# Down-weight block sums in earlier places, and the last rows' roots on GpSimd, in a hybrid decoder block

## The chip, the cores and the metric

The kernel runs on one core of one Trainium2 chip. The metric is device time in microseconds (us). A core has engines with a queue each: TensorE (PE; its weight loads are PEld), VectorE (DVE), ScalarE (ACT), GpSimd (POOL) and SyncE (SP), which issues nearly all DMAs here. Each engine works its queue in order; engines wait for each other by semaphores, so an instruction that waits holds everything behind it on its own queue.

## The reference

A decoder block on 1024 tokens of width 1024, in float32: an S5 branch and a stick-breaking attention branch, merged, then a SwiGLU feed-forward layer, and a last norm. The change touches the end of the feed-forward layer and the last norm:

```python
def rmsnorm(x, g):
    xf = x.astype(jnp.float32)
    xf = xf * lax.rsqrt(jnp.mean(xf * xf, axis=-1, keepdims=True) + RMS_EPS)
    return (xf * g.astype(jnp.float32)).astype(x.dtype)

        ffn = (jax.nn.silu(h @ w_ffn_gate[l]) * (h @ w_ffn_up[l])) @ w_ffn_down[l]
        x = x + g2 * ffn
    return rmsnorm(x, norm_f_g)
```

The hidden width is 2816, so the down weights are 2816 x 1024. `g2` is a row of 1024 numbers that scales the columns of the down weights.

## The kernel before

**Products.** Every float32 product is made of three: an operand is cast to a shorter float on ACT (its high half, L473), and what is left is taken off on DVE (its low half, L474); high times high, high times low and low times high are summed in PSUM. `operand` does this "split" for a tile of 128x1024.

**Strassen.** The feed-forward products run as one level of Strassen: seven products of sums of half blocks in place of eight. The hidden columns are worked in eleven pairs of 256. Pairs 0 to 9 take the seven products; the eleventh is done plainly (`plain`), and its part of the down product comes last, row by row.

**Gate and up** (`gate_up`, once for each of ten pairs). After a pair's seven products (PE, L1279), ACT makes the silu (L1263), DVE the product with up (L1264), POOL five sums of half tiles (L1270), and SP stores seven left operands of the down product in `hD` (L1273). The tiles named f1 that hold them are used again by operands of the down product, once these stores have read them.

**Blocks of down weights.** The right operands of the down product come from the weights: for each pair, two tiles of 128x1024 are loaded (L1354; for the first four pairs L1194), scaled by `g2` on POOL (L1355, L1195), and combined into five sums of 128x512 on POOL (`down_sums`, L1326). Two scaled quarters are stored as they are (L1321) and the five sums in three stores (L1328). This is called a block here. Ten blocks, 0 to 9, are needed. Blocks 0 to 3 are made during gate and up, at every second pair; blocks 4, 5 and 6 beside products 3 to 5 of the first step of the down product; blocks 7, 8 and 9 beside products 3 to 5 of the second.

**The down product** (`down`). It has three steps, with four, three and three pairs each (`STEPS`); block q belongs to pair q, so the second step needs blocks 4 to 6 and the third blocks 7 to 9. In each step run the seven products (the first step in the order 2, 3, 1, 6, 7, 5, 4, the others in 2, 4, 5, 3, 1, 6, 7). A product has four row groups, each with 3 matmuls for every pair, summed in one PSUM bank (L1396): 48 matmuls in the first step, 36 in the others. For each pair of each product one operand is loaded from `hD` (L1375) into one of seven stage tiles (wb four times, ws twice, wgs), and split into one of eight pairs of tiles (named wh, wl, wgh, wxh, f). So there are 28, 21 and 21 operands. The results are copied (L1400) or added (L1402) to accumulators, and in the third step POOL combines these (`closing`, L1362).

**The last rows.** For eight rows of 128 tokens (4 to 7, then 0 to 3) PE adds the eleventh pair's part (L1433), DVE adds the accumulators (L1435), ACT sums squares (L1445; for the last row in halves, L1437), `rstd_s` makes the root with six ACT instructions on 128x1 (Ln, Exp, and one Newton step of four, L494 to L499), and DVE scales the row (L1418), which SP stores. The last row is scaled in halves, on ACT (L1412) and DVE (L1413); its first half is multiplied by the norm's weights on POOL beforehand (L1441), and its Ln takes a bias from the first half's sum, made by two small instructions (L1440).

**What sets the order.** A scheduler places the instructions on each queue when the program is built, from a model of their times. `after(a, b)` only tells it to place a behind b; at run time nothing waits for it. So the code's loops say when a block may be placed, and the scheduler where its parts stand on SP, POOL, DVE, ACT and PE.

## Time and profile before

| | |
|---|---|
| time, median of 3 runs | 1471.52 us (1470.78 to 1475.69) |
| the profiled execution: time, span of its instructions | 1475.07 us, 1473.3 us |
| busy in the span: PE, DVE, ACT, POOL | 1413.9, 1094.9, 632.8, 507.1 us |
| first matmul of the down product | 1243.71 us |
| first matmul of its second and third step | 1321.96 and 1379.08 us |
| first matmul of the last rows | 1440.74 us |
| blocks 4 to 9 on POOL, start to end | 1256.9 to 1273.9, 1278.0 to 1293.9, 1293.9 to 1311.8, 1311.8 to 1328.8, 1345.2 to 1361.1, 1361.1 to 1376.1 us |

A row of the order of time has the start, the length, the engine and the line, the operation, out<-in with the program's tile names, and in brackets the idle time of the engine before it, with who ended it. "SPq" is the issue of a DMA on SP's queue. A row of a window has its bounds and length, then the busy time and count of PE, PEld, DVE, ACT and POOL, the granted clock of TensorE, the share of the DMA engines and GB/s (with one engine alone where a row is shorter). A row of a group ends with the busy time, the mean length in ns, and the idle time before. A row of DMA issues ends with the size of one and the median time to landing. A matmul of 128x512 shows as 0.39 us, since matmuls overlap; they start some 0.227 us apart.

### The profile page before, as it was taken

How to read it: one execution, taken by the hardware profiler on the slowest of the kernel's cores; microseconds unless marked ns; L12 is line 12 of the kernel's file. 1: busy time of each engine (PE TensorE's matmuls, PEld its weight loads, DVE VectorE, ACT ScalarE, POOL GpSimd, SP SyncE). 2: the span in 40 equal slices, each digit the busy share in tenths (PEclk: the TensorE clock that was granted, in tenths of full speed). 3: DMA queues.
4: the chain of work that ended last, by engine and by line, in shares of the span. 5: the costliest groups of instructions: out<-in, count | busy, mean ns of one | idle time of the engine just before them, and what ended most of it. 6: DMA issues, size and time to landing. Idle time of an engine off the chain costs nothing.

```text
span 1473.3 us, 18281 instructions
## 1 busy us (share of the span) xinstructions
PE 1413.9 (96%) x6730; PEld 1118.4 (76%) x6730; DVE 1094.9 (74%) x1424; ACT 632.8 (43%) x847; POOL 507.1 (34%) x265
## 2 busy tenths in 40 slices
PE   5898999999899999999999999999999999999997
PEld 3678988788666666668888788888888888788785
DVE  5778996356788888887723678777766667999797
ACT  3321121641586858675418543233323234433335
POOL 1000000001210122102400015877667563895694
PEclk9999999999999999999999999999999999999998
DMA  9546664569311111116452223644444358999732
GB/s 339 140 104 157 161 178 120 173 199 335 109 36 51 36 51 57 50 50 218 141 198 88 85 86 108 208 147 167 137 133 146 124 197 315 328 340 330 277 102 115
DMA packets 193561, 233.39 MB, mean 158 GB/s; under 512 B 29500, under 2 KB 128896, under 8 KB 193472
## 3 DMA queue, kind: packets, MB, share of 16 engines
q1 hardware_dynamic: 184336, 224.70, 46.9%
q10 hardware_dynamic: 8912, 7.48, 1.9%
q8 instruction: 53, 0.87, 0.3%
q14 instruction: 36, 0.29, 0.1%
q0 software_dynamic: 224, 0.05, 0.0%
HBM read 162.85 MB, written 68.16 MB: 157 GB/s over the span
## 4 chain that ended last, share of the span: by engine, by line
PE 69%; DVE 13%; DMA 6%; ACT 5%; issue 3%; POOL 3%; SPq 1%; DVEq 0%; ACTq 0%; POOLq 0%
PE tq L1279 12%; PE mm L1279 6%; PE wo L1279 6%; PE mx L812 5%; PE ga L738 4%; PE mm L812 4%; PE mm L738 3%; PE acc L812 2%; PE mm L1117 2%; PE mm L646 2%; PE mx L738 2%; PE z L812 2%; PE wo L1117 2%; PE tq L1396 2%; PE tq L1228 2%
## 5 line engine op out<-in xcount | busy, mean ns | idle before, releaser
L471 POOL TENSOR_TENSOR ws<-wb 128x1024 f32<-128x1024 f32 x24 | 61.6, 2568 | 174.0 <-DVE wl L474 150.2
L455 POOL TENSOR_TENSOR wl<-ws,wh 128x1024 fp32r<-128x1024 f32 x12 | 31.3, 2610 | 166.7 <-ACT wh L452 166.2
L905 DVE TENSOR_TENSOR wa<-wa,acc 128x512 f32<-128x512 f32 (+1 forms) x80 | 47.0, 628 | 32.6 <-ACT row L903 30.1
L1270 POOL TENSOR_TENSOR f<-f,f 128x512 f32<-128x512 f32 x30 | 53.2, 1797 | 37.9 <-DVE f L1264 32.6
L294 POOL MEMSET tz<- 128x1024 f32 x4 | 3.8, 953 | 179.1 <-PE mm L646 96.9
L1326 POOL TENSOR_TENSOR pa<-pa 128x512 f32<-128x512 f32 x30 | 62.3, 2109 | 0.2
L877 ACT ACTIVATE ws<-wa 128x1024 f32<-128x1024 f32 (+1 forms) x40 | 39.0, 976 | 48.7 <-DVE wa L874 43.5
L882 DVE TENSOR_TENSOR wl<-ws,wh 128x1024 fp32r<-128x1024 f32 (+1 forms) x40 | 57.1, 1427 | 1.0
L474 DVE TENSOR_TENSOR wl<-ws,wh 128x1024 fp32r<-128x1024 f32 x23 | 39.3, 1707 | 20.4 <-ACT wh L473 20.4
L1396 PE MATMUL tq<-f,f 128*128 128x512 f32 x156 | 47.5, 391 | 1.6 <-DVE f L474 1.5
L1355 POOL TENSOR_TENSOR pa<-pa,row 128x1024 f32<-128x1024 f32 x14 | 41.3, 2973 | 20.6 <-DMA pa<-in_w_ffn_down_dram 16.4
L1263 ACT ACTIVATE f<-f 128x1024 f32<-128x1024 f32 x20 | 21.2, 1061 | 62.9 <-DVE f L1299 32.2
L880 DVE SCALAR_TENSOR_TENSOR ws<-wa,ws 128x1024 f32<-128x1024 f32 (+1 forms) x40 | 45.5, 1137 | 2.9 <-ACT ws L879 2.0
L908 ACT ACTIVATE wa<-wa 128x1024 f32<-128x1024 f32 (+1 forms) x40 | 38.8, 971 | 19.5 <-DVE wa L905 18.5
L982 DVE SCALAR_TENSOR_TENSOR acc<-aw,cond,acc 128x512 f32<-128x512 f32 x56 | 41.8, 746 | 6.8 <-DMA aw<-in_w_ada_dram 6.1
L452 ACT CAST wh<-ws 128x1024 fp32r<-128x1024 f32 x24 | 25.1, 1049 | 49.7 <-PE wo L1117 22.4
L474 DVE TENSOR_TENSOR wl<-wb,wh 128x1024 fp32r<-128x1024 f32 x25 | 46.3, 1861 | 0.1
L812 PE MATMUL z<-q,k 64*128 64x512 f32 (+3 forms) x192 | 41.8, 526 | 4.1 <-DVE wa L874 2.9
L1279 PE MATMUL tq<-x,wh 128*128 128x512 f32 x144 | 44.4, 390 | 0.1
L1279 PE MATMUL tq<-pa,wh 128*128 128x512 f32 x144 | 44.3, 389 | 0.0
L473 ACT CAST wh<-ws 128x1024 fp32r<-128x1024 f32 x23 | 24.2, 1054 | 44.9 <-PE tq L1279 31.8
L471 POOL TENSOR_TENSOR wgs<-wb 128x1024 f32<-128x1024 f32 x12 | 28.9, 2407 | 42.2 <-DVE wl L474 21.1
(909 smaller groups left out, 4683.9 us busy)
## 6 DMA issues: line engine op xcount, KB each, us to landing
wb<-hD SPq DMA_DIRECT2D x40, 512.0 KB, 6.0
aw<-in_w_ada_dram SPq DMA_DIRECT2D x64, 256.0 KB, 4.4
hD<-f SPq DMA_DIRECT2D x30, 512.0 KB, 5.5
ws<-in_w_in_dram SPq DMA_DIRECT2D x23, 512.0 KB, 4.4
wb<-in_w_ffn_gate_dram SPq DMA_DIRECT2D x44, 256.0 KB, 4.2
wb<-in_w_ffn_up_dram SPq DMA_DIRECT2D x44, 256.0 KB, 4.8
ws<-hD SPq DMA_DIRECT2D x20, 512.0 KB, 5.4
x<-in_x_dram SPq DMA_DIRECT2D x16, 512.0 KB, 7.0
```

Of the source, the lines that this page charges most:

```text
L471: (add or nc.gpsimd).tensor_tensor(st, a, b, op)
L474: self.last_lo = (lo or nc.vector).tensor_tensor(l, a, h.bitcast(F32), ALU.subtract)
L738: self.nc.tensor.matmul(ps, lhsT=w[a][:, k], rhs=act[h][k][:, b], start=(j == 0), stop=(j == n - 1))
L812: return self.tc.keep_in_program_order(self.nc.tensor.matmul(*args, **kw))
L880: nc.vector.scalar_tensor_tensor(st, a, 0.0, st, ALU.max, ALU.add)
L882: nc.vector.tensor_tensor(lt, st, ht.bitcast(F32), ALU.subtract)
L905: nc.vector.tensor_tensor(a[:, x, 0:f], a[:, x, 0:f], r[:, x, 0:f], ALU.subtract)
L1117: self.nc.tensor.matmul(ps, lhsT=mg[t // 4][k][:, a, P * (t % 4):P * (t % 4) + P], rhs=ws[k // 2][b][:, k % 2], start=k + j == 0, stop=k + ...
L1270: self.last_sum = nc.gpsimd.tensor_tensor(o, a, b, op)
L1279: self.nc.tensor.matmul(ps, lhsT=w[x][:, q, k], rhs=self.B[i](y, k), start=(j == 0), stop=(j == 11))
L1326: self.after(nc.gpsimd.tensor_tensor(t[:, n], part(a), part(b), SIGN_B[i]), first)
L1396: nc.tensor.matmul(ps, lhsT=o[x][:, P * t:P * t + P], rhs=o[y][:, R], start=(j == 0), stop=(j == 3 * np_ - 1))
```

## The change

Three things change. Block 4 is placed in the last pair of gate and up: `ffn` keeps the silu of the pair before the last, and `down` makes the block ahead of everything else, placed behind that silu. Blocks 5 to 9 are made one at each product from the first step's fourth on, so 5 to 8 in the first step and 9 at the first product of the second, followed by the scaling of the eleventh pair's two weight tiles (which before came at the second step's sixth product). And for the last four rows the Newton step goes to POOL (`rstd_p`, three instructions in place of four on ACT), as do the two small instructions of the last row's bias; Ln and Exp stay on ACT.

```diff
+    def rstd_p(self, ss, y, h, b=None):
+
+        act, ts = self.nc.scalar.activation, self.nc.gpsimd.tensor_scalar
+        b, bh = b or (self.eps[:, 0:1], self.eps[:, 1:2])
+        act(y, ss, AF.Ln, bias=b, scale=1.0 / 1024.0)
+        act(y, y, AF.Exp, scale=-0.5)
+        ts(h, ss, -0.5 / 1024.0, bh, ALU.mult, ALU.add)
+        ts(h, h, y, y, ALU.mult, ALU.mult)
+        ts(y, h, 1.5, y, ALU.add, ALU.mult)
         return y
...
-            silu = self.silus[-1]
+            self.silu, silu = silu if j else None, self.silus[-1]
...
-        def weights(m):
+        def weights(m, first):
             w = self.PA.tile([P, 1024], F32, name="pa")
             nc.sync.dma_start(out=w, in_=w_v[m])
-            self.after(nc.gpsimd.tensor_tensor(w, w, g2, ALU.mult), self.last_lo)
+            self.after(nc.gpsimd.tensor_tensor(w, w, g2, ALU.mult), first)
             return w
+
+        def block(q, first):
+            self.down_sums(q, [weights(2 * q + m, first) for m in range(2)], self.PA, "pa", [first] * 3)
+
+        block(STEPS[0], self.silu)
+        due = list(range(STEPS[0] + 1, sum(STEPS)))
...
-                if s < len(STEPS) - 1 and 2 <= n < 2 + STEPS[s + 1]:
-                    q = p0 + np_ + n - 2
-                    rows = [weights(2 * q + m) for m in range(2)]
-                    self.down_sums(q, rows, self.PA, "pa", [self.last_lo] * 3)
-                if s == len(STEPS) - 2 and n == 5:
-                    WL = [weights(20 + m) for m in range(2)]
+                if due and (s or n > 2):
+                    block(due.pop(0), self.last_lo)
+                    if not due:
+                        WL = [weights(20 + m, self.last_lo) for m in range(2)]
...
-                r = self.rstd_s(ss[:, 1:2], small[:, t, 2:3], small[:, t, 3:4], (small[:, t, 4:5], small[:, t, 5:6]))
+                r = self.rstd_p(ss[:, 1:2], small[:, t, 2:3], small[:, t, 3:4], (small[:, t, 4:5], small[:, t, 5:6]))
...
-            r = self.rstd_s(ss[:, 0:1], small[:, t, 2:3], small[:, t, 3:4])
+            r = (self.rstd_p if t < 4 else self.rstd_s)(ss[:, 0:1], small[:, t, 2:3], small[:, t, 3:4])
...
-                            nc.scalar.activation(small[:, t, n:n + 1], ss[:, 0:1], AF.Identity, bias=self.eps[:, n - 4:n - 3], scale=f / 1024.0)
+                            nc.gpsimd.tensor_scalar(small[:, t, n:n + 1], ss[:, 0:1], f / 1024.0, self.eps[:, n - 4:n - 3], ALU.mult, ALU.add)
```

Up to the last pair of gate and up every queue is as before. Behind it the scheduler places much anew. Line numbers of the changed kernel are 11 to 17 higher: L1392 there is L1375, L1365 is L1354 or L1355 with its multiply at L1366, L1332 is L1321, L1339 is L1328, L1356 is L1345.

SP's queue in the last pair, before: operand loads (wb, ws from `hD`) and the accumulators' first values (pb from `xD` and `cD`).

```order
L1345 DMA pb<-xD 128x2x512 x4
L1375 DMA ws<-hD 128x1024
L1345 DMA pb<-cD 128x1024 x2
L1375 DMA wb<-hD 128x1024
L1345 DMA x_9927<-xD 128x2x512
L1345 DMA x_9928<-xD 128x2x512
```

The same place now:

```order
L1356 DMA pb<-xD 128x2x512 x2
L1332 DMA hD<-pa 128x512
L1356 DMA pb<-xD 128x2x512 x2
L1332 DMA hD<-pa 128x512
L1392 DMA ws<-hD 128x1024
L1365 DMA pa<-in_w_ffn_down_dram 128x1024 x2
L1356 DMA pb<-cD 128x1024
L1339 DMA hD<-pa 128x2x512
L1356 DMA pb<-cD 128x1024
L1339 DMA hD<-pa 128x2x512
L1392 DMA wb<-hD 128x1024
L1339 DMA hD<-pa 128x512
```

Block 4's five stores (hD<-pa) and the loads of block 5's weights stand among these loads. The loads of block 4's weights stood ahead of this place before as well.

SP's queue where the third step's first operands are loaded, before. The first row loads block 9's weights. The next two loads of wb are that step's first and second operand; its third is the first wb of the last row. Between them stand block 8's sums (three stores of L1328), block 9's quarters (L1321), block 9's first sums (L1328) and the eleventh pair's weights (L1354).

```order
L1354 DMA pa<-in_w_ffn_down_dram 128x1024 x2
L1375 DMA wb<-hD 128x1024
L1328 DMA hD<-pa 128x2x512
L1375 DMA wb<-hD 128x1024
L1328 DMA hD<-pa 128x2x512
L1328 DMA hD<-pa 128x512
L1321 DMA hD<-pa 128x512 x2
L1354 DMA pa<-in_w_ffn_down_dram 128x1024
L1328 DMA hD<-pa 128x2x512
L1354 DMA pa<-in_w_ffn_down_dram 128x1024
L1375 DMA ws<-hD 128x1024
L1375 DMA wb<-hD 128x1024 x2
```

The same place now, from block 9's first quarter on; the third step's first operands are the loads of wb behind the eleventh pair's weights (L1365).

```order
L1332 DMA hD<-pa 128x512
L1392 DMA ws<-hD 128x1024
L1392 DMA wgs<-hD 128x1024
L1332 DMA hD<-pa 128x512
L1365 DMA pa<-in_w_ffn_down_dram 128x1024 x2
L1339 DMA hD<-pa 128x2x512
L1392 DMA wb<-hD 128x1024
L1339 DMA hD<-pa 128x2x512
L1392 DMA wb<-hD 128x1024
L1339 DMA hD<-pa 128x512
L1392 DMA wb<-hD 128x1024 x2
```

Block 9's stores still stand between these loads, but the block itself is made beside the second step's first product.

POOL's queue at the end, now. Before, only the multiply of pa by gf (L1441 there) stood behind the last `closing`.

```order
L510 TENSOR_SCALAR ss_11533<-ss_11533 128x1
L508 TENSOR_SCALAR ss_11533<-ss_11533,eps 128x1
L509 TENSOR_SCALAR ss_11533<-ss_11533 128x1
L510 TENSOR_SCALAR ss_11533<-ss_11533 128x1
L1455 TENSOR_SCALAR ss_11533<-ss_11533,eps 128x1 x2
L1456 TENSOR_TENSOR pa<-pa,gf 128x512
L508 TENSOR_SCALAR ss_11533<-ss_11533 128x1
L509 TENSOR_SCALAR ss_11533<-ss_11533 128x1
L510 TENSOR_SCALAR ss_11533<-ss_11533 128x1
```

The last row's three refining instructions (L508 to L510) stand behind the multiply of its first half.

More of the change, by code (lines that the diff above doesn't have):

```diff
@@ L499, in rstd_s @@
         self.nc.scalar.mul(y, y, h)
+        return y
+    def rstd_p(self, ss, y, h, b=None):
[6 more added lines that the diff above has]
+        ts(y, h, 1.5, y, ALU.add, ALU.mult)
         return y
```

## The prediction

> **What bounds the kernel now.** I read the page's chain first, then the busy time by stage with the stages cut where the first matmul of each begins, then the order of time on each engine around the two stages that are too long, and last the tail.
>
> ```profile
> PE 69%; DVE 13%; DMA 6%; ACT 5%; issue 3%; POOL 3%; SPq 1%; DVEq 0%; ACTq 0%; POOLq 0%
> 1205.60:1243.71 38.11, 38.11 (x169) 31.53 (x168) 22.14 (x26) 11.97 (x14) 14.31 (x8) 1.00 0.96 342
> 1243.71:1321.90 78.19, 76.69 (x337) 62.90 (x336) 75.11 (x50) 33.95 (x38) 70.89 (x30) 1.00 0.90 319
> 1321.90:1379.08 57.18, 57.18 (x254) 47.34 (x253) 49.77 (x47) 17.59 (x18) 40.78 (x20) 1.00 0.82 286
> 1379.08:1440.70 61.62, 59.71 (x253) 48.21 (x252) 53.96 (x51) 22.77 (x23) 47.45 (x26) 0.97 0.51 177
> 1440.70:1462.66 21.96, 21.96 (x97) 17.83 (x96) 19.74 (x25) 16.17 (x48) 11.11 (x8) 1.00 0.28 112
> 1462.66:1473.30 10.64, 0.00 (x0) 0.00 (x0) 3.87 (x4) 5.38 (x22) 1.75 (x1) 0.65 0.43 166
> ```
>
> The chain runs through PE for 69% of the span. The windows (length, then busy time with count of PE, weight loads, DVE, ACT and POOL, clock, DMA share, GB/s) are the last gate and up pair, the three steps of the down product, the last rows, and the tail. Matmuls and their order count as equal work: the steps have 336, 252 and 252. The second step has PE busy throughout, so 57.18 / 252 = 0.2269 us is the pace. The first step should then take 336 x 0.2269 = 76.24 and takes 78.19: **1.95 us** lost. The third should take 57.18 and takes 61.62: **4.44 us** lost. The rows lose nothing. The tail, 10.64 us without a matmul, is what is left. So at most some 6.4 us of PE waits lie in the reach of the change, and a part of the tail.
>
> **The third step's wait.** Where the 4.44 us lie, on PE, with the clock beside it:
>
> ```profile
> 1380.21 0.39 PE L1396 MATMUL mm<-wgh,wgl 128*128 128x512 f32 x1
> 1381.68 0.50 PE L1396 MATMUL mm<-wxh 128*128 128x512 f32 x1 [1.08 <-ACT wxh L473]
> 1382.94 0.50 PE L1396 MATMUL mm<-wxl,wxh 128*128 128x512 f32 x1 [0.76 <-DVE wxl L474]
> ...
> 1389.26 0.40 PE L1396 MATMUL tq<-wh 128*128 128x512 f32 x1
> 1384.00:1386.00 2.00, 2.00 (x6) 0.50 1.06 425
> 1380.58 1.04 ACT L473 CAST wxh<-wb 128x1024 fp32r<-128x1024 f32 x1 [16.02 <-DMA wb<-hD]
> ```
>
> The third operand (wxh, wxl) comes late, and the granted clock falls to 0.50 behind the two gaps. From 1380.21 the matmul at 1389.26 is the 22nd in the program; at the pace it stands at 1380.21 + 22 x 0.2269 = 1385.20. So this place costs 4.06 us. ACT had waited 16.02 us for the operand's load. Why the load was late stands on SP's queue and on POOL:
>
> ```profile
> 1284.18 0.39 SPq L1375 DMA_DIRECT2D wb<-hD  x1
> ...
> 1372.34 0.37 SPq L1328 DMA_DIRECT2D hD<-pa  x1
> 1373.32 0.78 SPq L1375 DMA_DIRECT2D ws<-hD  x1
> 1374.15 0.95 SPq L1375 DMA_DIRECT2D wb<-hD  x2
> 1345.18 5.77 POOL L1355 TENSOR_TENSOR pa<-pa,row 128x1024 f32<-128x1024 f32 x2 [16.40 <-DMA pa<-in_w_ffn_down_dram]
> 1361.11 6.73 POOL L1355 TENSOR_TENSOR pa<-pa,row 128x1024 f32<-128x1024 f32 x2
> 1367.81 8.27 POOL L1326 TENSOR_TENSOR pa<-pa 128x512 f32<-128x512 f32 x5
> ```
>
> SP issues in order. The store of block 9's first pair of sums went out only at 1372.34, when POOL had made them (its sums run from 1367.81), and the operand loads queued behind it follow at 1373.32 and 1374.15, some 5 us before the step begins. POOL was late because it had stood idle 16.40 us for block 8's weights. **Not POOL's load but the place of the last two blocks holds PE here.**
>
> The change puts blocks 5 to 8 beside products 4 to 7 of the first step and block 9 beside the first product of the second. I count a block on POOL as 17 us, from block 4 now:
>
> ```profile
> 1246.70 5.76 POOL L1270 TENSOR_TENSOR f<-f,f 128x512 f32<-128x512 f32 x3 [24.90 <-DVE f L1264]
> ...
> 1256.89 5.80 POOL L1355 TENSOR_TENSOR pa<-pa,row 128x1024 f32<-128x1024 f32 x2
> 1262.65 11.20 POOL L1326 TENSOR_TENSOR pa<-pa 128x512 f32<-128x512 f32 x5
> pa<-in_w_ffn_down_dram SPq DMA_DIRECT2D x14, 512.0 KB, 5.9
> ```
>
> Scaling and sums of block 4 take 5.80 + 11.20 = 17.0 us. In the change block 5 takes this place (its weights are loaded in the last pair), to 1273.9. Block 6's loads stand behind the operand loads of the sixth product, of which the last (the 24th operand's) goes out at 1284.18 now, the first row above; with 5.9 us of landing block 6 runs some 1290 to 1307, and 7, 8 and 9, if none waits again, to 1324, 1341 and 1358. The third step's third operand is then loaded near 1358, some 20 us ahead instead of 5. I take **-4.1 us** here: the whole place, clock included, but not the 0.4 us of small pauses later in the step, for which I have no cause. What is late next is nothing in the second step, whose own loads move behind sums by up to 6 us at most, against a lead of some 10 us: the loads are issued when stages come free, one product and seven stages ahead.
>
> **The block in the last pair** fits the 24.90 us in which POOL waits: 17.0 us from about 1221.8 end near 1239, before 1246.70, when L1270 starts. It is nothing on POOL. On SP its stores stand ahead of the eighth operand's load and hold that one some 6 us, and block 5's two loads come forward too. PE's new order does not need that operand before 1268. On DVE it makes the splits slower while POOL works:
>
> ```profile
> 1234.24 1.21 DVE L474 TENSOR_TENSOR wl<-wb,wh 128x1024 fp32r<-128x1024 f32 x1
> ...
> 1249.01 2.31 DVE L474 TENSOR_TENSOR f<-ws,f 128x1024 fp32r<-128x1024 f32 x1
> ...
> 1255.70 0.68 DVE L1400 COPY x<-mm 128x512 f32<-128x512 f32 x1
> ...
> 1265.93 2.31 DVE L474 TENSOR_TENSOR f<-wb,f 128x1024 fp32r<-128x1024 f32 x1
> 1268.29 1.67 PE L1396 MATMUL tq<-f,f 128*128 128x512 f32 x6 [1.50 <-DVE f L474]
> ```
>
> The same split takes 1.21 with POOL idle and 2.31 with POOL at a block. In the last pair DVE is busy 22.14 of 38.11 us, and the three or four splits in that stretch get 1.1 us longer each: covered, as PE is full there (38.11) and these operands belong to the next stage. If that cover is gone, it is 3 to 4 us.
>
> **The first step's wait** is the last row: PE waits for the low half of the eighth operand, which DVE ends at 1268.24. The new order has PE and DVE take the third product's operands first. Counting down the new DVE order from 1249.01 (the sixth operand's split, a PSUM copy whose bank is done at 1253.9, then the splits of operands 9, 10, 12, 11, 13 and 7 at 2.3 us each, with one more copy of 0.6 after the first), the seventh operand's low half ends near 1268.7, and PE wants it at 1243.71 + 107 x 0.2269 = 1268.0. The eighth ends near 1271 and is wanted near 1271.5. So about 0.7 of the 1.95 us stay: **-1.2 us**, with bounds 0 and -1.95, and a loss of a few us if the loads in the last pair land late.
>
> **The tail.** Let T be 1462.66.
>
> ```profile
> 1462.70 0.69 DVE L1435 TENSOR_TENSOR pa<-tq,pb 128x512 f32<-128x512 f32 x1 [0.51 <-PE tq L1433]
> 1463.20 0.61 ACT L1437 ACTIVATE ft<-pa 128x512 f32<-128x512 f32 x1
> 1464.55 0.61 ACT L1437 ACTIVATE ft<-pa 128x512 f32<-128x512 f32 x1
> 1465.29 0.29 ACT L494 ACTIVATE ss<-ss 128x1 f32<-128x1 f32 x1
> 1467.06 0.29 ACT L499 ACTIVATE ss<-ss 128x1 f32<-128x1 f32 x1
> 1467.44 0.72 ACT L1412 ACTIVATE pa<-pa,ss 128x512 f32<-128x512 f32 x1
> 1467.98 0.75 DVE L1413 SCALAR_TENSOR_TENSOR pa<-pa,ss,gf 128x512 f32<-128x512 f32 x1
> 1463.99 1.75 POOL L1441 TENSOR_TENSOR pa<-pa,gf 128x512 f32<-128x512 f32 x1 [12.18 <-ACT ft L1437]
> L1125 POOL MEMSET eps<- 128x1 f32 x3 | 0.2, 93 | 0.0
> L454 POOL TENSOR_SCALAR wh<-ws 128x1024 fp32r<-128x1024 f32 x6 | 7.7, 1276 | 102.3 <-issue 36.1 <-PE mm L812 34.0 <-PE mx L812 32.2
> ```
>
> ACT is behind: the last half row is ready at 1463.39, its square starts at 1464.55. The change takes 18 activations of 128x1 off ACT (four for each of four rows, and the two of L1440) and gives POOL 14 of a kind that no row shows at that size. I bound one between 0.093 us (the 128x1 MEMSET) and 1.28 us (the TENSOR_SCALAR of 128x1024), and take 0.2, near the row of its own size. ACT then no longer lags: the last square starts near T + 0.75, Ln 0.74 later as now, Exp 0.4 after that, done at T + 2.1. POOL is the longer way: the first half's square ends near T + 0.6, two small ones, L1441's 1.75, which the new order puts ahead of the last root's three, three small ones and 0.1 for the handover: T + 0.6 + 0.4 + 1.75 + 0.6 + 0.1 = T + 3.45. The last DVE multiply now starts at 1467.98 = T + 5.32. That is **-1.8 us** (both multiplies start together; DVE's 0.75 and the stores stay). At 0.093 it is -2.4, at 1.28 it is T + 8.95, or +3.6.
>
> The Trainium skill (GPSIMD Engine Reference, 3.1) speaks against this move: GpSimd has two software dispatch hops where VectorE has one. Its measured 4497 ns for 2048 elements at 2.6 cycles of 1.2 GHz leaves, as an estimate from that page, some 0.06 us for an instruction's start, and by that the tail would gain 2.6 instead of 1.8. No run so far shows it.
>
> **Sum.** -4.1 - 1.2 - 1.8 = -7.1 us. The profiled execution took 1475.07 for a span of 1473.3, so 1468.0; against the median of 1471.52 of the runs shown, **1464.4**. 0.3% is 4.4 us, about what a measurement of this kernel can tell from no change.
>
> **Rivals.** (1) *The wait moves but stays*: SP still meets a store whose sums are not made, ahead of the third step's loads. For it speaks that every block is stored between operand loads; against it the 20 us of lead. It leaves -1.2 - 1.8 = -3.0: 1468.5. Chance 0.13. (2) *Small GpSimd instructions are dear*, over 0.9 us each: the tail loses 2 to 3.6, in all -4.1 - 1.2 + 2.8 = -2.5: 1469. Chance 0.12. (3) *The last pair's DMA is full*: it has a share of 0.96 at 342 GB/s, and block 4's and 5's 1 MB of loads and 1.75 MB of stores there are 8 us more. The first step's operands come late, it loses 2 instead of gaining 1.2: 1467.6. Chance 0.1. (4) *Slower*: POOL waits for weights again, as the 16.40 us show it can. The third operand's load must go out by about 1368, block 9 ends at 1273.9 + 4 x 17 = 1342 without waits, so 26 us of waits are free. With 16.4 for three of four blocks it ends at 1391, 23 us late, and of this the change's 7.1 comes off: 1471.5 + 16 = 1487. It is slower than before from 33 us of waits on. Chance 0.1.
>
> The Trainium skill (TensorE: Matmul & The Clock Gate, Part 1) has the clock fall only after an idle window of about 3.4 us. The trace differs: 0.50 behind gaps of 1.08 and 0.76. By the page a new short wait would cost its length alone; by the row some 1.8 us more.
>
> **Chances and range.** The forecast has 0.55. Faster by over 0.3% (under 1467.1): the forecast and a little of (3), 0.58. Within 0.3%: (1), (2) and most of (3), 0.31. Slower: (4) and a part of what I don't see, 0.11. The forecast's own range is 1462 to 1467; to hold 8 in 10 it must take in the three middle rivals: 1461.5 to 1471.5.
>
> **What would show it.** Right: the third step at 57.2 to 57.6 us with no clock under 1.00, POOL at block 4 before 1240, the first step near 77 us, L1441 ahead of three TENSOR_SCALAR of about 0.2 us, and 8.8 us from the last matmul to the end. Wrong: a PE wait for a split whose load follows a store on SP, POOL waiting over 26 us for weights in all, or small POOL instructions over half a microsecond.

## The result and the profile after

The changed kernel takes 1467.6 us (median; 1463.8 to 1469.5) where the kernel before, run beside it, takes 1475.6 (1468.6 to 1479.8). The ratio is 0.9949 with a 95% interval of 0.9931 to 0.9967: 7.5 us less, with 4.9 to 10.2 as the interval's ends. The profiled execution took 1467.38 us for a span of 1465.7.

The windows of the changed kernel, cut at the same places as those of the kernel before (last pair, three steps, last rows, tail; columns as there):

```profile
1204.11:1242.22 38.11, 38.11 (x169) 31.53 (x168) 24.11 (x26) 12.08 (x14) 27.26 (x15) 1.00 0.96 354
1242.22:1319.91 77.69, 76.40 (x337) 62.97 (x336) 68.70 (x53) 34.21 (x38) 59.66 (x27) 1.00 0.93 339
1319.91:1377.09 57.18, 57.18 (x254) 47.32 (x253) 54.07 (x51) 21.12 (x23) 42.10 (x16) 1.00 0.94 341
1377.09:1434.21 57.12, 57.12 (x254) 47.30 (x252) 50.87 (x48) 18.59 (x19) 48.83 (x28) 1.00 0.32 102
1434.21:1456.13 21.92, 21.92 (x97) 17.83 (x95) 17.34 (x22) 15.05 (x43) 8.81 (x12) 1.00 0.31 121
1456.13:1465.70 9.57, 0.00 (x0) 0.00 (x0) 3.08 (x4) 2.92 (x9) 4.46 (x9) 0.63 0.42 164
```

The length column is what to read. The third step is down by 4.50 us (61.62 to 57.12), the first by 0.50 (78.19 to 77.69), the tail by 1.07 (10.64 to 9.57). The last pair, the second step and the rows stand still to within 0.04. From the first matmul of the down product to the end it is 229.59 before and 223.48 now: **6.1 us**. The remaining 1.5 us of the two spans lie ahead of that matmul, where nearly all of the program is the same; they are taken up with the last two experiments.

Why the third step no longer waits, on SP, POOL and ACT of the changed kernel:

```profile
1286.18 5.00 POOL L1366 TENSOR_TENSOR pa<-pa,row 128x1024 f32<-128x1024 f32 x2 [14.93 <-DMA pa<-in_w_ffn_down_dram]
...
1355.43 6.74 POOL L1366 TENSOR_TENSOR pa<-pa,row 128x1024 f32<-128x1024 f32 x2
1355.90 0.96 SPq L1392 DMA_DIRECT2D wb<-hD  x2
1367.77 1.05 ACT L473 CAST wxh<-wb 128x1024 fp32r<-128x1024 f32 x1 [5.20 <-PE tq L1411]
```

POOL waits 14.93 us for block 6's weights, and then never again: the eleventh pair's scaling, behind block 9, starts at 1355.43. The load of the third operand goes out near 1356, and ACT casts it at 1367.77, some 9 us before the step begins at 1377.09. Before, that cast began at 1380.58, 1.5 us after the step had begun.

The one wait of PE in the down product now, the splits on DVE ahead of it, and block 5's scaling on POOL:

```profile
1253.38 6.72 POOL L1366 TENSOR_TENSOR pa<-pa,row 128x1024 f32<-128x1024 f32 x2
...
1257.77 3.42 DVE L474 TENSOR_TENSOR wxl<-ws,wxh 128x1024 fp32r<-128x1024 f32 x1
...
1265.57 2.30 DVE L474 TENSOR_TENSOR f<-wgs,f 128x1024 fp32r<-128x1024 f32 x1
1267.93 1.19 PE L1411 MATMUL tq<-f,f 128*128 128x512 f32 x4 [1.29 <-DVE f L474]
```

PE waits 1.29 us for the seventh operand's low half, which DVE ends at 1267.87. One split ahead of it, beside POOL's scaling, took 3.42 us instead of 2.3. The scaling that it met ended at 1260.10 (1253.38 + 6.72), 2.33 us after the split began; with the 1.22 of a split alone that makes 3.55.

The tail (T is the end of the last matmul, 1456.13), POOL and DVE:

```profile
1457.43 1.58 POOL L1455 TENSOR_SCALAR ss<-ss,eps 128x1 f32<-128x1 f32 x2
1458.97 1.26 POOL L1456 TENSOR_TENSOR pa<-pa,gf 128x512 f32<-128x512 f32 x1
1460.22 0.26 POOL L508 TENSOR_SCALAR ss<-ss 128x1 f32<-128x1 f32 x1
...
1457.44 1.28 DVE L1433 SCALAR_TENSOR_TENSOR pa<-pa,ss,gf 128x1024 f32<-128x1024 f32 x1 [0.27 <-POOL ss L510]
1461.32 0.75 DVE L1428 SCALAR_TENSOR_TENSOR pa<-pa,ss,gf 128x512 f32<-128x512 f32 x1 [2.59 <-POOL ss L510]
```

The last row's multiply (L1428) starts at T + 5.19, hardly before the T + 5.32 of the kernel before. The small POOL instructions of the root take 0.26 us, but the two that make the bias (L1455) take 1.58 together. From that multiply to the end it takes 4.38 us instead of 5.32, and there the rest of the 1.07 lies: before, DVE scaled the seventh row (L1418) right ahead of the last multiply, and its store went out just ahead of the last two; now that scaling ends 2.6 us ahead of the multiply. That this is the reason is argued from the rows; the kernel below that puts this scaling and its store last (5.64 us from the multiply to the end) speaks for it.

### The profile page after: what moved, and what is told of

The parts are those of the page before. It is cut to its first block, busy times and chain, and to the rows that moved or that the text cites. A ratio compares the mean times of both kernels' runs of the same rounds, so it can differ in the third digit from the quotient of the medians.

```text
span 1465.7 us, 18286 instructions
## 1 busy us (share of the span) xinstructions
PE 1410.2 (96%) x6730; PEld 1117.0 (76%) x6730; DVE 1091.1 (74%) x1424; ACT 628.8 (43%) x829; POOL 511.6 (35%) x279
## 4 chain that ended last, share of the span: by engine, by line
PE 76%; DVE 10%; DMA 6%; ACT 5%; issue 2%; SPq 0%; POOL 0%; ACTq 0%; POOLq 0%; DVEq 0%
PE tq L1290 13%; PE wo L1290 6%; PE mm L1290 6%; PE tq L1411 6%; PE mx L823 5%; PE ga L749 4%; PE mm L823 4%; PE wo L1411 3%; PE mm L1411 3%; DMA aw<-in_w_ada_dram 2%; PE acc L823 2%; PE mm L1128 2%; PE mm L657 2%; PE z L823 2%; PE wo L1128 2%
## 5 line engine op out<-in xcount | busy, mean ns | idle before, releaser
L1366 POOL TENSOR_TENSOR pa<-pa,row 128x1024 f32<-128x1024 f32 x14 | 43.7, 3135 | 14.9 <-DMA pa<-in_w_ffn_down_dram 14.9
L473 ACT CAST wh<-wb 128x1024 fp32r<-128x1024 f32 x25 | 26.2, 1051 | 40.1 <-PE tq L1290 19.1
```

The costliest lines, as they stand in the source:

```text
L473: nc.scalar.copy(h, a)
```

## The experiments

All stages below are lengths between the same matmuls as above. The third step is the one from which most came, so the first four kernels take the change apart.

**The tail alone** (`e1_tail_only`): the kernel before with this much of the change.

```diff
-                r = self.rstd_s(ss[:, 1:2], small[:, t, 2:3], ...
+                r = self.rstd_p(ss[:, 1:2], small[:, t, 2:3], ...
-            r = self.rstd_s(ss[:, 0:1], ...
+            r = (self.rstd_p if t < 4 else self.rstd_s)(ss[:, 0:1], ...
-                            nc.scalar.activation(small[:, t, n:n + 1], ...
+                            nc.gpsimd.tensor_scalar(small[:, t, n:n + 1], ...
```

> The kernel before with the roots of the last four rows and the two bias instructions on GpSimd, the blocks where they were. Theory (each part of the change acts for itself): only the tail shortens, by the 1.1 us seen between the two profiles, so about -1 us in all; the third step stays near 61.6 us, the first near 78.2, the tail comes to 9.6. Rival (the gain is the tail's, and the rest is a difference between executions): -4 us or more.

**The blocks alone** (`e2_blocks_only`): the changed kernel with these lines undone.

> The changed kernel with all roots and the two bias instructions on ScalarE again, as before. Theory: the blocks bring the third step to 57.2 us and the first to 77.7, the tail stays at 10.6: -5 us against before. Rival (the stages after shift the wait into the rows or the tail once the tail is not relieved): the rows or the tail get longer by over 1 us and the gain is under -4.

The third step and the tail of the first, then of the second kernel (windows), and the last multiply of the second:

```profile
1378.08:1439.98 61.90, 58.27 (x253) 47.06 (x252) 53.97 (x51) 22.77 (x23) 47.33 (x26) 1.00 0.50 176
1461.91:1472.20 10.29, 0.00 (x0) 0.00 (x0) 3.77 (x5) 3.58 (x11) 4.55 (x9) 0.70 0.42 165
```

```profile
1374.18:1431.30 57.12, 57.12 (x253) 47.30 (x252) 50.90 (x48) 18.58 (x19) 48.83 (x28) 1.00 0.33 104
1453.23:1463.10 9.87, 0.00 (x0) 0.00 (x0) 4.83 (x4) 4.63 (x19) 1.27 (x1) 0.76 0.41 160
...
1457.80 0.75 DVE L1428 SCALAR_TENSOR_TENSOR pa<-pa,ss,gf 128x512 f32<-128x512 f32 x1
```

The tail alone is worth nothing that can be measured: the ratio is 0.9997 (0.9980 to 1.0013), and the tail is 0.35 us shorter than before, not 1.1. The blocks alone have a ratio of 0.9942 (0.9924 to 0.9961). Their third step is 57.12, and the tail is 0.77 us shorter with all roots on ACT. So most of what the tail gained is the blocks' doing, and the move of the roots is worth 0.30 to 0.35 us. Both expectations had this wrong by the same 0.7. With the blocks alone the multiply starts at T + 4.57 (1457.80 - 1453.23), with 5.30 from there to the end; the roots on POOL put it off by 0.62 and shorten what follows by 0.92.

The first kernel also shows what the lower clock is worth. Its third step has the same two gaps in the same place, then a third one; the last row here is of the kernel before:

```profile
1380.81 0.51 PE L1407 MATMUL mm<-wxh 128*128 128x512 f32 x1 [1.22 <-ACT wxh L473]
1382.07 0.50 PE L1407 MATMUL mm<-wxl,wxh 128*128 128x512 f32 x1 [0.75 <-DVE wxl L474]
1391.90 0.73 PE L1407 MATMUL tq<-f 128*128 128x512 f32 x2 [1.60 <-ACT f L473]
1390.80 1.04 ACT L473 CAST f<-ws 128x1024 fp32r<-128x1024 f32 x1 [4.18 <-DMA ws<-hD]
...
1391.55 1.05 ACT L473 CAST f<-ws 128x1024 fp32r<-128x1024 f32 x1 [3.93 <-DMA ws<-hD]
```

The granted clock stays at 1.00 behind gaps of 1.22 and 0.75 us, where it fell to 0.50 behind 1.08 and 0.76 in the kernel before. The step is no shorter for it: PE runs ahead and then waits 1.60 us for a later operand, whose load (ws) is late too. In the kernel before, ACT casts that operand just as late (12.5 us into the step, here 12.7), and PE, slowed by the clock, comes there as it gets ready. So late loads set the length of this step in both, the third operand's and this one's, and the low clock added nothing to it that shows.

How the blocks reach the tail, in the last rows of the kernel before:

```profile
1445.77 6.04 POOL L1362 TENSOR_TENSOR pb<-pb,x 128x512 f32<-128x512 f32 x4
1450.51 2.38 DVE L1418 SCALAR_TENSOR_TENSOR pa<-pa,ss,gf 128x1024 f32<-128x1024 f32 x1
```

POOL was still at the closing sums (L1362), to 1451.81, 11 us into the rows; two row scalings on DVE beside them took 2.02 and 2.38 us instead of 1.28, and DVE's row additions ran late from there on. With the blocks alone POOL ends these sums at 1437.39, 6.1 us into the rows, and the scalings all take 1.28 until the sixth row's (2.28, beside POOL's multiply). The next two kernels leave the roots on ACT and agree: with block 4 alone POOL ends these sums 11.1 us into the rows, and the tail is 10.7; with the last three blocks alone 6.6 us into them, and the tail is 9.9.

**Block 4 alone** (`e3_block4_only`): the kernel before with block 4 in the last pair; the others in their old places.

```diff
+        block(STEPS[0], self.silu)
...
-                if s < len(STEPS) - 1 and 2 <= n < 2 + STEPS[s + 1]:
+                if s < len(STEPS) - 1 and 2 + (not s) <= n < 2 + STEPS[s + 1]:
```

> The kernel before with only block 4 moved into the last gate and up pair; blocks 5 and 6 stay at the fourth and fifth product of the first step, 7 to 9 in the second step. Theory (the place of the last two blocks on SyncE's queue holds the third step): the third step keeps its wait, 61.2 to 61.6 us; the first step gains what comes from an unloaded GpSimd, at most 0.5 without the new order of its operands; so 0 to -0.5 us. Rival (GpSimd's load as a whole, from block 4 on, makes the last blocks late): the third step loses most of its 4.4 us, -3 us or more.

**The last three blocks alone** (`e4_late_blocks_earlier`): the kernel before with blocks 7 to 9 two products earlier.

```diff
-                if s < len(STEPS) - 1 and 2 <= n < 2 + STEPS[s + 1]:
-                    q = p0 + np_ + n - 2
+                if s < len(STEPS) - 1 and 2 - 2 * s <= n < 2 - 2 * s + STEPS[s + 1]:
+                    q = p0 + np_ + n - 2 + 2 * s
```

> The kernel before with only blocks 7 to 9 two products earlier, at the first three products of the second step; block 4 stays in the first step. Theory: this alone takes away the third step's wait, 57.2 to 57.6 us, -4.1 us in all; the first step stays at 78.2. Rival (the block in the last pair is needed, because GpSimd comes too late otherwise): the third step still waits for its third operand, over 59 us, and the gain is under 2 us.

The third step's window and the cast of its third operand, of block 4 alone:

```profile
1375.55:1433.37 57.82, 57.69 (x253) 47.14 (x252) 53.01 (x51) 21.04 (x22) 45.78 (x25) 1.00 0.47 165
1373.57 1.05 ACT L473 CAST wxh<-wb 128x1024 fp32r<-128x1024 f32 x1 [12.54 <-DMA wb<-hD]
```

and of the last three blocks alone:

```profile
1379.55:1436.67 57.12, 57.12 (x254) 47.30 (x253) 53.25 (x51) 19.74 (x20) 50.20 (x27) 1.00 0.38 123
1370.22 1.06 ACT L473 CAST wxh<-wb 128x1024 fp32r<-128x1024 f32 x1 [5.21 <-PE tq L1396]
```

The last three blocks do what was expected: 57.12 and a cast 9.3 us ahead of the step (1379.55 - 1370.22), as in the changed kernel. The first step stays at 78.09. The ratio is 0.9942 (0.9923 to 0.9960). But block 4 alone takes the wait away as well, which the theory excluded: 57.82, though blocks 7 to 9 stand where they stood. What is left, 0.7 us, are small pauses 9.7 to 11.3 us into the step at the same later operand from ws as above, which ACT casts at 1384.18 after 3.82 us without its load. POOL's chain then ends 3 us earlier against the step, and the cast comes 2.0 us ahead of it, still released by the load. Its ratio is 0.9961 (0.9944 to 0.9979). So POOL's chain was only some 3 us too late, and either a shorter chain or an earlier place mends it; the earlier place leaves a lead of 9 us.

**The bias instructions back on ACT** (`e5_bias_act`): the changed kernel with

```diff
-                            nc.gpsimd.tensor_scalar(small[:, t, n:n + 1], ...
+                            nc.scalar.activation(small[:, t, n:n + 1], ...
```

> The changed kernel with the two bias instructions of the last row back on ScalarE; the roots stay on GpSimd. T is the end of the last matmul; in the profile of the changed kernel the last row's multiply starts at T + 5.2, and at T + 4.6 where all roots stay on ScalarE. Theory (the two bias instructions, 1.58 us together, sit ahead of GpSimd's multiply and of Ln and hold both): the multiply starts near T + 3.7, 1.5 us earlier. Rival (the three small instructions of the root behind GpSimd's multiply are what is long): it starts later than T + 4.6, and the time is that of the changed kernel.

**The seventh row's scaling last** (`e6_row7_late`): the changed kernel with

```diff
+            if t == ROWS[-2]:
+                held.append((t, row, r))
+                return
             nc.vector.scalar_tensor_tensor(row, row, r, gf, ALU.mult, ALU.mult)
...
         close(*last)
+        for t, row, r in held:
+            self.after(nc.vector.scalar_tensor_tensor(row, row, r, gf, ALU.mult, ALU.mult), self.final)
+            nc.sync.dma_start(out=out[:, t], in_=row)
```

where `final` is the last row's multiply.

> The changed kernel with VectorE's scaling of the seventh row placed behind the last row's multiply, so that VectorE does nothing while GpSimd works on the last row. Theory (a GpSimd instruction that meets a VectorE instruction with all its operands in SBUF waits for its end): the two bias instructions take 0.5 to 0.7 us together instead of 1.58, and the last row's multiply starts near T + 4.3 instead of T + 5.2; the end gains nothing, since the seventh row's store of 512 KB now goes out last, 1.3 us later. Rival (a GpSimd instruction with a second tensor operand is simply long, 0.8 us): they stay at 1.58 and the multiply at T + 5.2.

The tail of the first of these (its T is 1458.40):

```profile
1459.71 2.32 DVE L1433 SCALAR_TENSOR_TENSOR pa<-pa,ss,gf 128x1024 f32<-128x1024 f32 x1 [0.27 <-POOL ss L510]
1463.01 0.75 DVE L1428 SCALAR_TENSOR_TENSOR pa<-pa,ss,gf 128x512 f32<-128x512 f32 x1 [0.97 <-POOL ss L510]
1459.69 1.26 POOL L1456 TENSOR_TENSOR pa<-pa,gf 128x512 f32<-128x512 f32 x1
1460.93 1.23 POOL L508 TENSOR_SCALAR ss<-ss 128x1 f32<-128x1 f32 x1
```

and of the second (its T is 1457.25):

```profile
1458.55 0.50 POOL L1458 TENSOR_SCALAR ss<-ss,eps 128x1 f32<-128x1 f32 x2
1461.36 0.75 DVE L1428 SCALAR_TENSOR_TENSOR pa<-pa,ss,gf 128x512 f32<-128x512 f32 x1 [3.06 <-POOL ss L510]
```

With DVE idle beside them, the same two bias instructions take 0.50 us instead of 1.58, and the multiply starts at T + 4.11. So they were long because of DVE's scaling: in the changed kernel it starts at 1457.44, 0.01 us behind the first of them, and ends at 1458.72, and POOL is done just behind it, at 1459.01. As expected the end gains nothing: the tail is 9.75, since the seventh row's store now goes last.

With the bias on ACT the multiply starts at T + 4.61, earlier than T + 5.19 but not at the T + 3.7 that was expected, and the tail is 9.0 instead of 9.6: moving the bias to POOL had cost 0.6 us. The rows show the cause from both sides. POOL's multiply started 0.02 us ahead of DVE's scaling: it took its 1.26, and the scaling 2.32. Behind it POOL's first root instruction, 0.26 elsewhere, took 1.23 and ended 0.13 us after the scaling. In the kernel before it is DVE that came first, by 0.66 us:

```profile
1463.33 1.28 DVE L1418 SCALAR_TENSOR_TENSOR pa<-pa,ss,gf 128x1024 f32<-128x1024 f32 x1
```

It took its 1.28, and POOL's multiply behind it (1463.99, in the prediction) 1.75 instead of 1.26. So the one that comes first keeps the other out. Start times 0.01 us apart do not tell who came first: the first bias instruction of the changed kernel is stamped 1457.43, the scaling 1457.44, and it was the bias that waited. The Trainium skill states this (SBUF — State Buffer, "SBUF: two separate sides"): GpSimd and a VectorE instruction with two SBUF inputs share a pair of ports, and who starts first holds it for the whole instruction. The traces agree, and the rule would have priced both the bias instructions and the splits of the first step.

**The last row's root on DVE** (`e7_dve_root`): the bias on ACT as above, and

```diff
-    def rstd_p(self, ss, y, h, b=None):
+    def rstd_p(self, ss, y, h, b=None, eng=None):
-        act, ts = self.nc.scalar.activation, self.nc.gpsimd.tensor_scalar
+        act, ts = self.nc.scalar.activation, (eng or self.nc.gpsimd).tensor_scalar
...
-                r = self.rstd_p(..., (small[:, t, 4:5], small[:, t, 5:6]))
+                r = self.rstd_p(..., (small[:, t, 4:5], small[:, t, 5:6]), nc.vector)
```

> The changed kernel with the last row's three root instructions on VectorE and its two bias instructions on ScalarE; rows 0 to 2 keep their roots on GpSimd. Theory (GpSimd's queue is what the last row waits for): the multiply starts near T + 3.3, the tail falls from 9.6 to 7.7 us, -1.9 against the changed kernel. Rival (the tail is bound by the stores, 2.8 us behind their issue, and by ScalarE's chain): the multiply starts no earlier than T + 4.5 and the tail stays above 9 us.

Its T is 1460.29:

```profile
1461.60 2.32 DVE L1433 SCALAR_TENSOR_TENSOR pa<-pa,ss,gf 128x1024 f32<-128x1024 f32 x1 [0.27 <-POOL ss L510]
1464.70 0.75 DVE L1428 SCALAR_TENSOR_TENSOR pa<-pa,ss,gf 128x512 f32<-128x512 f32 x1
```

Between the two: the multiply starts at T + 4.41, not T + 3.3, and the tail is 8.81. The scaling met POOL's multiply again and took 2.32; without that 1.04 it would have been T + 3.37, as an estimate.

The ratios to the kernel before of these three are 0.9959 (0.9937 to 0.9980), 0.9970 (0.9953 to 0.9988) and 0.9941 (0.9924 to 0.9959). The first and the last overlap widely with that of the change (0.9931 to 0.9967), so differences of a microsecond in the tail are read from the rows alone.

**All blocks one product later** (`e9_block5_late`):

```diff
-                if due and (s or n > 2):
+                if due and (s or n > 3):
```

> The changed kernel with blocks 5 to 9 one product later each: 5 to 7 at the fifth to seventh product of the first step, 8 and 9 at the first two of the second. GpSimd then has no block beside VectorE's splits of the sixth to fourteenth operand. Theory (the 1.3 us that PE still waits in the first step come from those splits, 2.3 us each beside a block and 1.2 without): the splits there take 1.2 us, the wait is gone and the first step takes 76.3 to 76.6 us instead of 77.7; the third step's third operand is still ahead, at 57.1. Rivals: the split waits for its operand's load and not for VectorE, and the first step stays at 77.7; or the blocks come too late again and the third step takes over 58.5 us.

The second step's window, PE's waits in it, and POOL ahead of block 6:

```profile
1323.10:1383.66 60.56, 57.80 (x254) 47.19 (x253) 57.95 (x53) 21.95 (x23) 44.83 (x20) 1.00 0.94 344
1334.47 0.50 PE L1411 MATMUL mm<-wh 128*128 128x512 f32 x1 [1.16 <-ACT wh L473]
1337.73 0.49 PE L1411 MATMUL mm<-wl,wh 128*128 128x512 f32 x1 [1.60 <-DVE wl L474]
1296.69 5.82 POOL L1366 TENSOR_TENSOR pa<-pa,row 128x1024 f32<-128x1024 f32 x2 [22.27 <-DMA pa<-in_w_ffn_down_dram]
```

This missed what it was made for. The scheduler left block 5's loads in the last pair, so POOL worked beside the same splits, and the first step stayed at 77.71: nothing follows for its wait. The other blocks did come later. POOL stood 22.27 us without weights, and a wait arose in the **second** step, at operands whose loads stand behind stores and loads of blocks; that step takes 60.56 instead of 57.18. One product later gives 3.4 of the 6.1 us back; the ratio is 0.9980 (0.9956 to 1.0003).

**Block 5 held back** (`e10_block5_held`): the changed kernel with a block's weight loads placed behind its product's operand loads.

```diff
-            nc.sync.dma_start(out=w, in_=w_v[m])
+            ins = nc.sync.dma_start(out=w, in_=w_v[m])
+            if ld is not None:
+                self.after(ins, ld)
...
-                    nc.sync.dma_start(out=st.rearrange(...), in_=self.hD[p0 + p, :, SLOT[i]])
+                    ld = nc.sync.dma_start(out=st.rearrange(...), in_=self.hD[p0 + p, :, SLOT[i]])
...
-                    block(due.pop(0), self.last_lo)
+                    block(due.pop(0), self.last_lo, ld)
```

> The changed kernel with block 5's two loads placed behind the 16th operand's load on SyncE, so that GpSimd begins block 5 some 10 us later (near 22 us into the first step instead of 11) and no longer works beside VectorE's splits of the sixth to twelfth operand. The loads of each later block are placed behind their product's operand loads in the same way, where they stood mostly already. Theory (the 1.3 us that PE still waits in the first step come from the splits, 2.3 to 3.4 us beside the block and 1.2 without): the splits there take 1.2 us, PE's wait is gone, and the first step takes 76.3 to 76.6 us instead of 77.7; the third step stays at 57.1. Rival (the split that PE waits for is late because of the cast or the load ahead of it): the splits get shorter, but the first step stays at 77.5 or more.

Its first step, a split there, and the start of block 5:

```profile
1244.32:1320.42 76.10, 76.10 (x337) 63.04 (x336) 67.51 (x53) 34.43 (x38) 58.80 (x27) 1.00 0.95 347
1258.07 1.22 DVE L474 TENSOR_TENSOR wgl<-wb,wgh 128x1024 fp32r<-128x1024 f32 x1 [0.55 <-ACT wgh L473]
1265.73 4.75 POOL L1368 TENSOR_TENSOR pa<-pa,row 128x1024 f32<-128x1024 f32 x2 [8.25 <-DMA pa<-in_w_ffn_down_dram]
```

With POOL done with the last pair's own sums at 1257.5 and idle until 1265.73, 21 us into the step, the splits between take 1.22 us, PE does not wait at all, and the first step is 76.10: 1.6 us less than with the change. The third step stays at 57.12. So without POOL beside them the splits are short and the wait is gone. But this kernel does not part the two alone: the scheduler also changed the order. The seventh operand's split stands one place further ahead on DVE, two splits run ahead of the first PSUM copy instead of behind it, and PE's matmuls stand in another order. That the long splits are enough to make the wait can be estimated from the changed kernel: its cast of wxh ends at 1257.10, and four splits of 1.22 from there would end the seventh operand's low half near 1262, over 4 us before PE wants it. Whether the new order would have been enough as well was not tried. The ratio is 0.9946 (0.9926 to 0.9966).

**Both, and nothing on POOL beside the seventh row's scaling** (`e11_held_dve`): block 5 held back, the last row's root on DVE and its bias on ACT together, and

```diff
-                        nc.gpsimd.tensor_tensor(row[:, cs], row[:, cs], gf[:, cs], ALU.mult)
...
-                nc.scalar.mul(row[:, L], row[:, L], r)
-                nc.vector.scalar_tensor_tensor(row[:, R], row[:, R], r, gf[:, R], ALU.mult, ALU.mult)
                 for cs in (L, R):
+                    nc.vector.scalar_tensor_tensor(row[:, cs], row[:, cs], r, gf[:, cs], ALU.mult, ALU.mult)
                     nc.sync.dma_start(out=out[:, t, cs], in_=row[:, cs])
```

> The same blocks, and in the tail the last row's root and both its multiplications on VectorE (GpSimd's multiplication of its first half left out as its own step, since VectorE's instruction multiplies by both factors), the bias instructions on ScalarE. Theory (VectorE and GpSimd shut each other out): with no GpSimd instruction beside it the seventh row's scaling takes 1.28 us again instead of 2.32; the root is ready near T + 3.4, the two multiplications end at T + 4.1 and T + 4.9, and the tail takes 8.4 us against 8.8 with only the root on VectorE. Rival (the scaling is long for another reason): it stays at 2.3, and the tail at 9.2 or more. In all, with the first step: -3 us against the changed kernel.

Its tail (T is 1456.99):

```profile
1458.29 1.28 DVE L1434 SCALAR_TENSOR_TENSOR pa<-pa,ss,gf 128x1024 f32<-128x1024 f32 x1 [0.27 <-POOL ss L510]
1460.37 1.42 DVE L1430 SCALAR_TENSOR_TENSOR pa<-pa,ss,gf 128x512 f32<-128x512 f32 x2
```

The scaling takes 1.28 again, the two multiplications run from T + 3.38 to T + 4.80 as expected, and the tail is 7.71, better than the 8.4 expected. From the first matmul of the down product to the end it is 220.04 us. The ratio to the kernel before is 0.9937 (0.9911 to 0.9963).

**The changed kernel and this one again, side by side** (`e12_after_again`, `e13_held_dve_again`; no edit).

> The changed kernel once more, beside the next one on the same chip. From the first matmul of the down product to the end it took 223.5 us in its first profile, against 229.6 before. Theory (the stages of the down product repeat, and what lies ahead of them varies by some us from execution to execution): 223 to 224 us again, first step 77.7, third 57.1, tail 9.6; in all -6 to -8 us against before. Rival (the stages themselves vary): one of these differs by over 0.5 us.

> The kernel with block 5 held back and the last row's root and multiplications on VectorE once more. It took 220.0 us from the first matmul of the down product to the end in its first profile. Theory: 220 us again, first step 76.1, third 57.1, tail 7.7; the median is 3 to 4 us under that of the changed kernel. Rival (what the stages gain is lost in the spread of what lies ahead): the medians of the two lie within 1.5 us.

The sum of the windows from the first matmul of the down product to the end, of the one and of the other:

```profile
sum 223.54, PE 212.66 PEld 175.41 DVE 194.67 ACT 91.90 POOL 163.82; mean PE 42.53 PEld 35.08 DVE 38.93 ACT 18.38 POOL 32.76
```

```profile
sum 220.04, PE 212.32 PEld 175.49 DVE 195.15 ACT 91.75 POOL 157.99; mean PE 42.46 PEld 35.10 DVE 39.03 ACT 18.35 POOL 31.60
```

The stages repeat to a tenth of a us: 223.48 and 223.54, 220.04 twice. The medians do not tell the two apart, against what was expected of the second: 1465.2 (1463.7 to 1466.9) and 1465.9 (1459.9 to 1471.6), ratios to the kernel before of 0.9934 (0.9909 to 0.9958) and 0.9933 (0.9911 to 0.9954). What lies ahead varies more than the 3.5 us between them: over the profiles of this study the down product began between 1239.28 and 1246.36, though its program up to the last pair is the same in all. So the shorter down product is shown by the stages, and not as a faster kernel. The 1.5 us ahead of the down product in the first pair of profiles lie well inside this spread, and the 6.1 us of the stages lie inside the interval of the measured ratio. What the spread comes from was not tried.

## Why the prediction was right, and where it was not

**The sum.** It gave -7.1 us; the stages show -6.1, the measured ratio -7.5. That 7.1 and 7.5 lie so close is in part luck: the third step gave 0.4 more than its term, the first step and the tail 0.7 less each, and 1.5 us lie ahead of the down product, in the spread of the last two experiments. The predicted 1464.4 is 3.2 under the measured 1467.6 because it was set against the first median of 1471.5; beside the changed kernel the kernel before took 1475.6, and 7.1 off that is 1468.5. So 1467.6 is in the range, but above the forecast's own 1462 to 1467. The direction, the bulk and its place were right. The windows are cut up to 0.06 us ahead of a step's first matmul (1321.90 for 1321.96), so a step of 252 matmuls without a wait takes 57.12, not 57.18, and one of 336 takes 76.16, not 76.24; the terms move by a tenth at most.

**The third step's wait (-4.1).** Right: -4.50. The 0.4 us of small pauses, kept because I had no cause for them, went too, here and wherever blocks 7 to 9 came earlier. They have the same cause: they stand 13.9 to 15.2 us into the step, at the later operand from ws whose load was late. The share given to the clock, 1.8 of the 4.06, was not one of its own: with the tail alone changed the clock stayed at 1.00 and the step took 61.90. One sentence was too strong: "Not POOL's load but the place of the last two blocks holds PE here." Block 4 alone, which leaves that place as it is, takes the wait away with a lead of 2 us. The load counts as well; the place only counts for more (9 us). The lead was forecast at 20 us from load to step, and it is 21 (1356 to 1377.09). The 9 us that are named above are from the cast to the step.

**The block in the last pair.** Right. POOL's rows there, block 4 and then the pair's sums:

```profile
1220.28 5.75 POOL L1366 TENSOR_TENSOR pa<-pa,row 128x1024 f32<-128x1024 f32 x2
1225.99 7.29 POOL L1337 TENSOR_TENSOR pa<-pa 128x512 f32<-128x512 f32 x5
1245.16 5.77 POOL L1281 TENSOR_TENSOR f<-f,f 128x512 f32<-128x512 f32 x3 [11.88 <-DVE f L1275]
```

It is done at 1233.28, with 11.88 us to spare, and the last pair keeps its 38.11. It took 13.0 us, not 17: the five sums took 1.46 us each, where beside the splits they take 2.24 (11.20 / 5 in the kernel before).

**The first step's wait (-1.2).** It fell by 0.5. The step that failed is the row of splits "at 2.3 us each": the six took 14.9 us and not 13.8, one of them 3.42 and one 2.81, and the seventh operand's low half ended at 1267.87, not 0.7 but 1.3 us after it was wanted. The price was read as a slowdown, and is an exclusion: a split waits for the POOL instruction that it meets, so its length hangs on what that is (here scalings of 128x1024 rather than sums of 128x512). The kernel with block 5 held back has short splits and no wait; since its order is another too, POOL's part is shown to be enough for the wait by estimate, and not by a kernel that changes nothing else.

**The tail (-1.8).** It is -1.07, and the mechanism was wrong. (At 1.28 us each the sum gives T + 8.85, not the T + 8.95 of the prediction.) By the sum the multiply would start at T + 0.6 + 0.4 + 1.75 + 0.6 + 0.1 = T + 3.45. It starts at T + 5.19: 1.30 until POOL is free of the seventh row's root (0.6 for the first half's square, which itself ended only at T + 1.20), 1.54 for the bias (taken as 0.4), 1.25 for POOL's multiply (1.75), 1.06 for the root (0.6), 0.04 (0.1). Where nothing shuts them out, the small instructions are 0.26 to 0.34 long, near the 0.2 taken, but start 0.36 to 0.44 apart, which is what the sum pays; the term left out is DVE's scaling beside them. "DVE's 0.75 and the stores stay" failed too, to the good: from the multiply to the end it is 0.94 us less, with the seventh row's store out of the way of the last two. Taken apart by kernels instead, 0.77 of the 1.07 are the blocks' (POOL's closing sums out of the way of the rows) and 0.30 the roots'. With the bias left on ACT the roots would have been worth 0.9 (9.9 to 9.0).

**The rivals.** The wait that moves but stays did not come. Dear small instructions came in a part: up to 1.35 us each where DVE holds them out, not in general; small instructions of over half a microsecond were named ahead as a sign of being wrong, and for the tail they were one. The last pair's DMA, 0.96 busy as before, cost nothing. The slower case did not come, but its mechanism is real and near: one product later POOL stood 22.27 us without weights and the second step lost 3.4. The forecast that a new short wait costs 1.8 us by a lower clock did not hold: behind 1.29 alone, behind 1.16 and 1.60 that lie 1.6 us of matmuls apart, and behind 1.22 and 0.75 with a single matmul between them, the granted clock stayed at 1.00.

## What to carry to other kernels

When an engine waits at a step's start, look for the load that came last, what stood ahead of it in its queue, and by how many us that was late: 3 us too late and 9 us ahead were here two products apart, and with all blocks one product later than in the change a wait was back in another step. When a wait goes away, look for the next late load behind it: where the clock did not fall, PE waited here for a later operand instead. Before work is moved from ScalarE to GpSimd, look at what VectorE does in the same microseconds: an instruction that takes 0.26 us alone takes as long as the VectorE instruction that it meets. And where a program's early part varies by some us from execution to execution, compare stages between the same instructions, which here repeat to a tenth of a us, beside the whole time.

## What the runs showed of the hardware

- GpSimd and a VectorE instruction that reads two tensors in SBUF take turns. The same VectorE scaling of 128x1024 took 1.28 us alone and 2.32 when GpSimd's multiply started 0.02 us ahead of it; the same GpSimd instruction of 128x1 took 0.26 and 1.23; a VectorE split took 1.22 alone, 2.3 beside GpSimd's sums and 3.42 when it met a scaling. A VectorE copy out of PSUM was not held: 0.69 us at 1254.43 of the changed kernel, in the middle of a scaling.
- A TENSOR_SCALAR of 128x1 takes 0.26 to 0.34 us on GpSimd when nothing holds it, with starts 0.36 to 0.44 us apart. On VectorE it took 0.20 to 0.27, with starts 0.30 to 0.31 us apart.
- The granted clock fell to 0.50 behind two gaps of 1.08 and 0.76 us with a single matmul between them (the third step before), and stayed at 1.00 behind two of 1.22 and 0.75 in the same place of the same step (the kernel with the tail alone), and behind gaps of 1.16 and 1.60 with 1.6 us of matmuls between (the kernel with all blocks one product later). So the lengths of the gaps do not tell whether it falls; what does was not tried.
